# One list of single-engine steps for the norm stage and the first 17 products of a diffusion-transformer layer

## The chip, the cores and the metric

The kernel runs on one core of a Trainium2 chip. A core has TensorE (matrix products, PE in the profile; its weight loads are PEld), VectorE (DVE), ScalarE (ACT), GpSimd (POOL) and SyncE (SP, which here issues the DMA transfers). Each engine takes its instructions strictly in the order in which they were written for it and waits on semaphores for the others. The metric is the device time of one execution in microseconds (us); lower is better.

## The reference

One layer of a backbone over 1024 latent tokens and 256 context tokens, width 1024, float32. The part that matters here is the beginning:

```python
sh1, sc1, gt1, sh2, sc2, gt2 = [m[:, None] for m in adaln(c, w_mod[l], b_mod[l])]
csh1, csc1, cgt1, csh2, csc2, cgt2 = adaln(c_ctx, w_mod[l], b_mod[l])
h = modulate(rmsnorm(x, g_pre1[l]), sh1, sc1)
q, k, v, f, g_a, g_f = split_proj(h @ w_in[l])
```

`adaln` is `silu(c) @ w_mod + b_mod`, split in six; `rmsnorm` scales each token by the inverse root of its mean square; `modulate` is `h * (1 + scale) + shift`. Attention with a window, a Fourier branch, a merge and a gated feed-forward network follow.

## The kernel before

**Tiles.** A tile is 128 partitions by 512 float32, 256 KB. There are 40 such buffers of one tag (`s`, line 61), which hold x, the weights, the modulated activations and the halves of the operands; 8 PSUM banks (line 442); and ten tiles of three tile widths (`ha`), in which first the rows of `w_mod` (`ws`) lie, later the operands B21, T2, T3, T4n and B22. Until an operand is written its tile is lent to the weights of the six later modulation groups (`wa`, line 740).

**Products.** `h @ w_in` is done with Strassen-Winograd products, seven for each pair of output blocks. An operand on the activation side is a quarter of h, transposed (B11, B21, B22), or a difference of quarters (T1, T2, T3, T4n); on the weight side a quarter (A11 to A22) or a sum (S1 to S4). A float32 operand goes to TensorE as a high half (a cast by ScalarE, `copy`) and a low half (the remainder, a subtraction by VectorE); three matmuls of 128x512 replace one (`mm3`, line 83). A product has four K tiles, so 12 matmuls. The products have numbers: 0 to 2 are P1 of three weight pairs (operand B11), 3 to 5 P2 (B21), 6 to 8 P5 (T1), 9 to 11 P6 (T2), 12 to 14 P7 (T3), 15 and 16 P4 and P3 of the first pair (T4n, B22). P1, P6 and P7 of a pair add up in one PSUM bank (X), copied out after each; P5 and P3 use a bank Y, P2 a bank Z.

**The start, step by step.**
- `x_load` (line 477) loads two tiles per 128 tokens; `x_square` (502) squares and sums them on ScalarE; `x_norm` (511) makes the inverse root for two token tiles: two operations on VectorE, a root on ScalarE, five operations on VectorE; `x_scale` (536) scales a tile, on VectorE or ScalarE.
- `x_turn` (542) transposes one K tile of half the tokens on TensorE, four transposes into one bank.
- `wm_stage` (487) loads a quarter of the first 2048 columns of `w_mod`, eight transfers; `mod_rows` (569) multiplies them by `silu(c)`; `mod_copy` (577) copies the bank; `mod_turn` (582) turns it into columns; `mod_vec` (598) makes shift and scale for the latent (`c` = 0) or context (`c` = 1) stream, three small operations on VectorE.
- `x_mod` (551) modulates a turned K tile (`hr`), on VectorE or ScalarE; `x_put` (560) splits it into halves of an operand.
- `pre` loads weight quarters, `sums` adds them, `conv` splits them, `mm` does the matmuls (a range of K tiles), `evac` copies a bank out and `after` does what follows from it (sigmoid, store).
- `ada_load`, `ada_rows`, `ada_copy` (735 to 756) do a later group of modulation rows: 8 transfers, 16 matmul instructions, one copy. `warm` (591) fills waits of TensorE with transposes that nothing reads.

**What sets the order.** All of this is in a block with `tc.manual_schedule()` (lines 905 to 1129): each engine gets its instructions in the order of the calls. Helpers that touch two engines, such as `conv` and `x_put` (cast on ScalarE, then subtraction on VectorE), place both at once. Weight loads stand at the top (907 to 922), the rest in the order of the products. From product 17 on (`run(17, NI - 5)`, line 1130) a planner that simulates the engines orders the work.

Of the kernel before, what the change touches and what calls it, by code (L numbers as in the profile page):

```python
# [38 lines left out]

@with_exitstack  # L40
def block_kernel(ctx: ExitStack, tc: tile.TileContext, t: dict, out: bass.AP, dbg: dict):
# [469 lines left out]
    def x_norm(tk, fill=()):

        fill = list(fill)

        def between():
            if fill:
                fill.pop(0)()
# [6 lines left out]
        between()  # L524
        nc.vector.reciprocal(out=r, in_=sq)
        mul(n1, r, r)
        mul(n1, n1, v)
        between()
        nc.vector.tensor_scalar(out=n1, in0=n1, scalar1=-0.5, scalar2=1.5, op0=ALU.mult, op1=ALU.add)
        mul(r, r, n1)  # L530
        for t_ in range(2):
            xr_[tk + t_] = r[:, t_:t_ + 1]
        for f in fill:
            f()

    def x_scale(tk, h, eng):
        if eng is None:
# [37 lines left out]
            nc.tensor.matmul(modp[q][g:g + 32, :], sv32[:, k, :], wms[q, k], start=k < 4, stop=k >= 4, skip_group_check=True)
# [328 lines left out]
    run, lead, main, pre, conv, sums, mm, evac, after, st = wino(pairs, items, ps, hooks, seng=[nc.vector])  # L904
    with tc.manual_schedule():
        V = nc.vector
        for tk in range(4):
# [3 lines left out]
        pre(1, ("A11",))
        pre(2, ("A11",))
        wm_stage(1)
        for tk in range(4, 8):
            x_load(tk)
        wm_stage(2)
        for j in range(2):
            pre(j, ("A21", "A22"))
        wm_stage(3)
        for j in range(3):  # L920
            pre(j, ("A12",))
        pre(2, ("A21", "A22"))
        hb.update(hb_tiles(hbp, [o for o in OPS if o not in hb], 10))
        mov.update(moving(hb))

        for tk in range(2):
            x_square(tk)
        x_norm(0)
        for tk in range(2, 4):
            x_square(tk)  # L930
        for i in range(2):
            for tk in range(2):
                x_scale(tk, i, V)
        for k in range(4):
            x_turn(0, k, range(2))
        x_norm(2)
        mod_rows(0, range(4))
        for tk in range(2, 4):
            x_scale(tk, 0, V)
        for k in range(4):  # L940
            x_turn(0, k, range(2, 4))
        conv(0, "P1")
        for tk in range(2, 4):
            x_scale(tk, 1, V)
        mod_rows(0, range(4, 8))
        mod_copy(0)
        warm(6)
        mod_turn(0)
        mod_vec(0, 0)
        warm(8)  # L950
        for k in range(2):
            x_mod(0, k, V if k else None)
        mod_vec(0, 1)
        for k in range(2):
            x_put("B11", k, hraw[0, k])
        mm(0, range(2))
        conv(1, "P1")
        mm(1, range(2))
        conv(2, "P1")
        mod_rows(1, range(8))  # L960
        ada_load(0, range(KT))
        mod_copy(1)
        mm(2, range(2))
        mod_turn(1)
        mod_vec(1, 0)
        for k in range(2, 4):
            x_mod(0, k, V if k % 2 else None)
        x_turn(0, 4)
        x_turn(0, 5)
        mod_vec(1, 1)  # L970
        for k in range(2, 4):
            x_put("B11", k, hraw[0, k])
        warm(8)
        mm(0, range(2, 4))
        x_square(4)
        x_square(5)
        mm(1, range(2, 4))
        x_norm(4)
        for tk in (4, 5):
            x_scale(tk, 0, V)  # L980
        mm(2, range(2, 4))
        mod_rows(2, range(4))
        x_square(6)
        x_square(7)
        x_norm(6)
        for tk in (6, 7):
            x_scale(tk, 0, V)
        for j in range(3):
            evac(j)
        mod_rows(2, range(4, 8))  # L990
        ada_load(1, range(KT))
        mod_copy(2)
        for k in range(2):
            x_turn(1, k)
        mod_turn(2)

        def t1(k):
            sub(hraw[0, k], hraw[1, k], hraw[0, k])
            x_put("T1", k, hraw[0, k])

        for k in range(2):
            x_mod(1, k)
        mod_vec(2, 0)
        for k in range(2):
            x_mod(0, k + 4, V)
        for k in range(2, 4):
            x_turn(1, k)
        sums(0, "S1")
        for k in range(2):
            t1(k)  # L1010
        conv(0, "P5")
        sums(1, "S1")
        mod_rows(3, range(4))
        for k in range(2, 4):
            x_mod(1, k)
        mod_vec(2, 1)
        conv(1, "P5")
        mm(6, range(2))
        for k in range(2, 4):
            t1(k)  # L1020
        x_turn(0, 6)
        x_turn(0, 7)
        mm(7, range(2))
        for k in range(2):
            x_put("B21", k, hraw[0, k + 4])
        mod_rows(3, range(4, 8))
        ada_load(2, range(KT))
        rope_load()
        mod_copy(3)
        mm(6, range(2, 4))  # L1030
        mod_turn(3)
        mod_vec(3, 0)
        for k in range(2, 4):
            x_mod(0, k + 4, V if k % 2 else None)
        mm(7, range(2, 4))
        conv(0, "P2")
        mod_vec(3, 1)
        for k in range(2, 4):
            x_put("B21", k, hraw[0, k + 4])
        mm(3, range(2))  # L1040
        conv(1, "P2")
        for tk in range(4, 8):
            x_scale(tk, 1, None)
        mm(3, range(2, 4))
        conv(2, "P2")
        for k in range(4, 6):
            x_turn(1, k)
        sums(2, "S1")
        for k in range(4, 6):
            x_mod(1, k)  # L1050
        evac(3, True)
        mm(4)
        for k in range(6, 8):
            x_turn(1, k)

        def t2(k):
            sub(hraw[0, k], hraw[1, k + 4], hraw[0, k])
            x_put("T2", k, hraw[0, k])

        conv(2, "P5")  # L1060
        for k in range(2):
            t2(k)
        for k in range(6, 8):
            x_mod(1, k)
        evac(4, True)
        sums(0, "S3")
        sums(0, "S2")
        mm(5)
        for k in range(2, 4):
            t2(k)  # L1070
        conv(0, "P6")
        evac(5, True)
        mm(8)
        ada_rows(0, 0)
        ada_rows(0, 1)
        ada_copy(0)
        ada_load(3, range(KT))
        for j in range(1, 3):
            sums(j, "S3")
            sums(j, "S2")  # L1080
        mm(9)
        conv(1, "P6")
        conv(2, "P6")
        ada_rows(1, 0)
        ada_rows(1, 1)
        ada_copy(1)
        ada_load(4, range(KT))
        for j in range(4, 9):
            after(j)
        mm(10)  # L1090
        evac(9)
        ada_rows(2, 0)
        for k in range(4):
            sub(hraw[1, k], hraw[1, k + 4], hraw[1, k])
            x_put("T3", k, hraw[1, k])
        ada_rows(2, 1)
        ada_copy(2)
        ada_load(5, range(KT))
        mm(11)
        for j in range(3):  # L1100
            conv(j, "P7")
# [4 lines left out]
        mm(12)
        ada_rows(3, 0)
        ada_rows(3, 1)
        ada_copy(3)
        for k in range(4):  # L1110
            sub(hraw[0, k], hraw[0, k + 4], hraw[0, k])
            x_put("T4n", k, hraw[0, k])
        mm(13)
        ada_rows(4, 0)
        ada_rows(4, 1)
        ada_copy(4)
        mm(14)
        for k in range(4):
            x_put("B22", k, hraw[1, k + 4])
        for k in range(12, 15):  # L1120
            lead(k)
# [1120 lines left out]
```

## Time and profile before

| | us |
|---|---|
| median of 3 runs | 1343.81 (1343.79 to 1344.8) |
| the profiled execution | 1343.85 |
| its span in the profile | 1342.1 |
| mean granted clock of TensorE | 0.985 |
| DVE busy in the span | 1041.7 |
| ACT busy in the span | 679.0 |
| bytes moved from 0 to 134 us | 34.85 MB |

Times in the views are counted from the start of the span; 1.75 us of the profiled execution lie outside it. "Granted clock" is the share of full speed at which TensorE's array ran. In a timeline row the first number is the start, the second the duration; bracketed is the idle time of that engine before the row and what ended it. Durations of matmuls overlap, so the step from one start to the next is the better price.

### The profile page before, as it was taken

To read this page: it belongs to the slowest core of one execution; us is meant where nothing else is said; L and a number is where in the kernel's file an instruction comes from. 1 tells how busy PE (TensorE), PEld (TensorE's weight loads), DVE (VectorE), ACT (ScalarE), POOL (GpSimd) and SP (SyncE) were. 2 spreads that over 40 slices of the span, in tenths; PEclk is the share of its full clock that TensorE was granted. 3 is DMA by queue.
4 is the path that set the end of the run, shared out by engine and by line. 5 is a ranking of instruction groups with operands and counts; after the bars stand their busy time and mean duration, and the time that the engine had idled before them with its cause. 6 is when DMAs were issued, how large, how long until landed. Compare 5 with 4: busy or idle time off the path is not lost.

```text
span 1342.1 us, 18506 instructions
## 1 busy us (share of the span) xinstructions
PE 1277.3 (95%) x5998; PEld 1029.8 (77%) x5998; DVE 1041.7 (78%) x1899; ACT 679.0 (51%) x1349; POOL 231.5 (17%) x191
## 2 busy tenths in 40 slices
PE   6887999999999999999999999999999999999996
PEld 3554877788888887777876888888888887888885
DVE  3665576879498898677789999989987887666767
ACT  4545334642466776435467554545454445534442
POOL 0000030210044334100000013444555200000000
PEclk9798999999999999999999999999999999999998
DMA  9946546450613335663422287868676568987884
GB/s 311 354 160 213 169 153 218 145 149 20 190 53 114 120 113 154 212 227 110 134 72 63 82 240 228 243 196 258 208 230 192 176 209 280 375 271 226 284 289 147
DMA packets 271572, 254.55 MB, mean 190 GB/s; under 512 B 16732, under 2 KB 206836, under 8 KB 271476
## 3 DMA queue, kind: packets, MB, share of 16 engines
q1 hardware_dynamic: 271476, 253.38, 60.5%
q8 instruction: 47, 0.77, 0.2%
q14 instruction: 49, 0.40, 0.1%
HBM read 179.65 MB, written 73.40 MB: 189 GB/s over the span
## 4 chain that ended last, share of the span: by engine, by line
PE 69%; DVE 15%; ACT 6%; DMA 4%; issue 3%; SPq 1%; POOL 1%; DVEq 0%; ACTq 0%; POOLq 0%
PE X_u L87 5%; PE X_u L85 5%; PE X_u L86 5%; PE Y_u L85 3%; PE X_d L86 3%; PE X_d L87 3%; PE X_d L85 3%; PE Y_u L86 3%; PE Y_u L87 3%; PE X_g L85 2%; DVE p L1308 2%; PE X_g L86 2%; PE X_g L87 2%; DVE pl L68 2%; PE Y_d L85 1%
## 5 line engine op out<-in xcount | busy, mean ns | idle before, releaser
L68 DVE TENSOR_TENSOR lP_u<-A_u,hP_u 128x512 fp32r<-128x512 f32 x132 | 107.0, 815 | 23.0 <-ACT hP_u L307 21.3
L369 ACT COPY snP_u<-X_u 128x512 f32<-128x512 f32 x57 | 33.4, 586 | 131.7 <-PE X_u L87 131.6
L369 ACT COPY snP_d<-X_d 128x512 f32<-128x512 f32 x48 | 28.2, 587 | 98.5 <-PE X_d L87 95.2
L307 ACT CAST hP_u<-A_u 128x512 fp32r<-128x512 f32 x121 | 74.6, 619 | 0.0
L1328 POOL TENSOR_SCALAR p<-p,sm 128x640 f32<-128x640 f32 (+1 forms) x64 | 48.3, 775 | 91.9 <-PE pp L1333 44.9
L80 ACT CAST ph<-pp 128x512 fp32r<-128x512 f32 x76 | 44.3, 584 | 22.5 <-PE pp L1333 21.2
L68 DVE TENSOR_TENSOR pl<-pp,ph 128x512 fp32r<-128x512 f32 x76 | 51.7, 681 | 2.5 <-ACT ph L80 2.0
L1322 ACT ACTIVATE p<-p,nm 128x640 f32<-128x640 f32 (+1 forms) x64 | 51.4, 803 | 0.7 <-DVE nm L1315 0.7
L68 DVE TENSOR_TENSOR yd<-yd,snP_d 128x512 f32<-128x512 f32 x36 | 24.9, 691 | 34.3 <-ACT snP_d L369 34.2
L68 POOL TENSOR_TENSOR A_u<-A_u,A_u 128x512 f32<-128x512 f32 x28 | 47.9, 1710 | 13.9 <-DVE lP_u L68 6.1
L1308 DVE CUSTOM_DVE_ANT_0 p<-ss,mask 128x640 f32<-128x640 f32 (+1 forms) x64 | 49.9, 782 | 0.0
L1333 PE MATMUL pp<-ident,p 128*128 128x128 f32 x304 | 46.6, 274 | 2.8 <-POOL p L1328 1.5
L1333 PEld LDWEIGHTS pp<-ident,p 128*128 128x128 f32 x304 | 37.2, 140 | 11.6 <-POOL p L1328 2.9
L1743 DVE SCALAR_TENSOR_TENSOR tb<-u,vec,tb 128x1024 f32<-128x1024 f32 x22 | 39.5, 1796 | 3.1 <-ACT tb L1740 3.1
L68 DVE TENSOR_TENSOR lP_g<-A_g,hP_g 128x512 fp32r<-128x512 f32 x48 | 33.3, 701 | 8.6 <-ACT hP_g L80 8.6
L68 POOL TENSOR_TENSOR S_u<-A_u,A_u 128x512 f32<-128x512 f32 x14 | 24.2, 1730 | 87.8 <-DMA g_d0P<-ghP 81.7
L1304 PE MATMUL ss<-kst,qs 128*128 128x384 f32 (+1 forms) x128 | 36.6, 367 | 1.3 <-DVE mx L1308 0.8
L1744 DVE SCALAR_TENSOR_TENSOR tb<-u,vec,tb 128x1024 f32<-128x1024 f32 x22 | 36.5, 1658 | 0.9
L68 POOL TENSOR_TENSOR A_u<-S_u,A_u 128x512 f32<-128x512 f32 x14 | 18.7, 1338 | 104.1 <-DVE lP_u L68 104.1
L68 DVE TENSOR_TENSOR wB<-wB,wB 128x512 f32<-128x512 f32 x44 | 36.0, 818 | 0.0
L1344 PE MATMUL po<-pl,vst 128*128 128x512 f32 x76 | 31.3, 412 | 2.3 <-DVE pl L68 1.7
L1747 ACT ACTIVATE tb<-tb 128x1024 f32<-128x1024 f32 x22 | 23.4, 1063 | 16.6 <-DVE tb L1744 16.5
(884 smaller groups left out, 4383.1 us busy)
## 6 DMA issues: line engine op xcount, KB each, us to landing
A_u<-in_w_up SPq DMA_DIRECT2D x88, 256.0 KB, 4.5
wB<-in_w_down SPq DMA_DIRECT2D x44, 256.0 KB, 4.3
wa<-in_w_mod SPq DMA_DIRECT2D x36, 256.0 KB, 5.3
wt_dT<-wB SPq DMA_DIRECT2D x33, 256.0 KB, 2.6
wdB<-in_w_down SPq DMA_DIRECT2D x33, 256.0 KB, 4.7
wdT<-wt_dT SPq DMA_DIRECT2D x33, 256.0 KB, 2.9
A_g<-in_w_in SPq DMA_DIRECT2D x32, 256.0 KB, 5.9
ws<-in_w_mod SPq DMA_DIRECT2D x30, 256.0 KB, 6.1
```

The costliest lines, as they stand in the source:

```text
L68: return (eng or nc.vector).tensor_tensor(out=out, in0=a, in1=b, op=op)
L80: copy(hi, src)
L85: nc.tensor.matmul(ps, ah, bh, start=start, stop=False, skip_group_check=True)
L86: nc.tensor.matmul(ps, ah, bl, start=False, stop=False, skip_group_check=True)
L87: nc.tensor.matmul(ps, al, bh, start=False, stop=stop, skip_group_check=True)
L307: copy(st[j]["half", p][0], st[j][STA[p]])
L369: copy(d["s" + p], d["X"])
L1308: nc.vector.tensor_tensor_reduce(out=p_, in0=ssc[:, lo:768], in1=self.mk, op0=ALU.add, op1=ALU.max, scale=1.0, scalar=-3.0e38, accum_out=s ...
L1322: nc.scalar.activation(out=self.pt[g], in_=self.pt[g], func=AF.Exp, scale=SCALE, bias=self.m[:, g:g + 1], accum_out=self.sm[:, g:g + 1])
L1328: nc.gpsimd.tensor_scalar(out=self.pt[g], in0=self.pt[g], scalar1=self.sm[:, g:g + 1], scalar2=1.0, op0=ALU.mult, op1=ALU.mult)
L1333: nc.tensor.transpose(pp[:, g * P:(g + 1) * P], self.pt[g][:, j * P:(j + 1) * P], ident)
L1743: nc.vector.scalar_tensor_tensor(out=tb, in0=u[:, 0:1024], scalar=cw[0], in1=tb, op0=ALU.mult, op1=ALU.add)
```

## The change

The block's body is replaced by a table of named steps and a list of 384 names, `START_ORDER`, that is walked once. Most steps issue work for one engine; with few exceptions (`na`, `ev`, `af`, `ld`, `mark`) a step has one engine, and the rest of a helper is a step of its own. `conv` becomes `ch` (cast, ScalarE) and `cl` (subtraction, VectorE); `x_put` becomes `h` and `l`, with the difference `dT` apart; `x_norm` becomes `na` and `nb`; `x_turn` comes in halves (`tn03a`: token half 0, K tile 3, first two token tiles); `mod_rows` in halves (`rw0a`), its loads by two (`wq00`); a product by K tiles (`mm2.0`). `sc` and `md` are scaling and modulation on VectorE, `sa` and `ma` on ScalarE; `ca` is `mod_copy` on ScalarE; `l112` loads weight quarter A11 of pair 2; `S10` is the sum S1 of pair 0; `al`, `ar`, `ac` are the later modulation groups; `ev` and `el` evacuate, `el` leaves out what follows, which `af` does; `ld` and `mark` do what the planner's products need ahead. The calls are those of before, on the same tiles. Nine scalings instead of twelve are on VectorE, three modulations instead of five, and none of the four copies of `mod_copy`.

```diff
+START_ORDER = """
+xl1 l112 xl0 sq00 sq01 sq10 ch2P1 sq11 wq00 xl2 sq20 sq21 na0 xl3 xl4 sq30 sq31 xl6 sq40 xl5 sq41 nb0 sa11 sq50 na2 
+sc00 sc10 tn03a wu6 nb2 sc20 sq51 sq60 sa30 tn01a sq61 tn00a na4 nb4 xl7 wu8 tn02a sq70 wu8 wq02 tn02b wq04 wq06 rw0a 
+wq10 rw0b sc31 sq71 na6 nb6 tn01b cl2P1 sc60 sa40 wq12 wq14 sc70 sa50 tn12a wq16 sc01 tn10a tn03b ca0 mt0 sa51 tn00b 
+sc71 mv00 ma01 ma00 tn12b tn10b tn13a tn13b sc21 mv01 tn11a tn11b md10 tn06a tn06b tn04a tn04b hB110 lB110 l110 dT10 
+hB111 lB111 wq20 wq22 wq24 rw1a ma11 rw1b ca1 ch0P1 mm2.0 dT11 wq26 mt1 cl0P1 mm2.1 l111 mv10 ma02 hB112 mv11 hT11 
+mm0.0 lB112 tn05a tn05b ma03 l220 mm0.1 mm0.2 hB113 md13 md12 l210 wq30 lB113 mm2.2 hT10 rw2a rw2b wq32 wq34 wq36 
+sa61 dT13 hb mm2.3 sa41 tn15a lT11 ca2 mt2 mv20 mm0.3 hT13 tn15b ch1P1 cl1P1 ma05 dT12 mm1.0 tn16a S10 hT12 mm1.1 
+l222 mm1.2 mm1.3 ma04 ch0P5 S30 tn14a tn14b tn16b l121 lT10 cl0P5 mm6.0 hB211 mv21 hB210 tn17a tn17b rw3a rw3b mm6.1 
+l120 l122 lT13 ma15 lB211 ma14 lB210 dT20 ev1 lT12 S20 ca3 mt3 l211 l212 hT20 lT20 ch0P6 ch1P2 mm6.2 mv30 mv31 cl1P2 
+mm6.3 al0 tn07a ma06 dT21 hB212 lB212 ch2P2 cl2P2 ma16 dT22 tn07b ma07 mm4.0 mm4.1 ev0 ma17 mm5.0 ch0P2 S12 S32 mm4.2 
+hT21 cl0P2 mm5.1 mm5.2 ch2P5 hB213 lB213 S22 l221 mm3.0 mm3.1 al1 al2 mm5.3 hB223 mm3.2 mm3.3 cl2P5 mm4.3 ch2P6 cl2P6 
+cl0P6 ev2 mm8.0 mm8.1 S11 dT23 ch2P7 mm9.0 lT21 mm9.1 dT41 hT22 mm8.2 mm8.3 el3 af4 mm11.0 S40 S31 ch1P7 lT22 el5 
+ch0P7 mm11.1 el4 af5 ar1a ar1b S21 ar0a ar0b hT23 lT23 dT32 ar2a ac0 ch1P6 dT43 ch1P5 hT4n3 dT33 hT33 mm11.2 mm9.2 
+mm9.3 dT31 al3 al4 mm11.3 cl1P6 mm10.0 mm10.1 hT31 al5 mm10.2 dT40 af6 af7 af8 cl1P5 mm7.0 mm7.1 ev9 mm7.2 ac1 cl0P7 
+ar2b ar3a S42 ar3b cl2P7 mm10.3 dT30 hT30 hT32 ac3 lT30 cl1P7 S41 mark ev10 ac2 mm7.3 mm12.0 rope mm13.0 ev11 dT42 
+mm14.0 lT31 mm14.1 lT32 mm14.2 lT33 lB223 mm12.1 mm12.2 mm14.3 mm12.3 lT4n3 ev12 mm13.1 ld12 mm13.2 ld13 hT4n0 lT4n0 
+hB220 lB220 ar5a ar4a hT4n1 lT4n1 hB221 hT4n2 ar4b ac4 ar5b mm13.3 mm15.0 mm15.1 mm16.0 lB221 mm16.1 hB222 lB222 
+mm16.2 lT4n2 ev13 mm15.2 mm16.3 ld14 ld15 ld16 ev14 mm15.3 ev15 ac5 ev16
+"""
...
-    def mod_copy(q):
+    def mod_copy(q, put):
         rows = s(f"mc{q}")
-        nc.vector.tensor_copy(rows, modp[q])
+        put(rows, modp[q])
...
-        for tk in range(4):
-            x_load(tk)
-        pre(0, ("A11",))
-        wm_stage(0)
...
-        for k in range(15, 17):
-            lead(k)
-            mm(k)
-            evac(k)
+        steps = {}
+
+        def step_(name, fn, *a):
+            steps[name] = lambda: fn(*a)
...
+        def put_hi(o, k, src):
+            copy(mov[o][0][k], hraw[src])
+
+        def put_lo(o, k, src):
+            sub(mov[o][1][k], hraw[src], fbits(mov[o][0][k]))
+
+        def diff(a, b, c):
+            sub(hraw[a], hraw[b], hraw[c])
+
+        def conv_hi(j, p):
+            nm = pairs[j][2]
+            st[j]["half", p] = (s(f"h{p}_{nm}", R), s(f"l{p}_{nm}", R))
+            copy(st[j]["half", p][0], st[j][STA[p]])
+
+        def conv_lo(j, p):
+            st[j][p] = hi, lo = st[j].pop(("half", p))
+            sub(lo, st[j][STA[p]], fbits(hi))
...
+            step_(f"ca{q}", mod_copy, q, lambda o, i: copy(o, i))
...
+        for name in START_ORDER.split():
+            steps[name]()
     run(17, NI - 5)
```

More of the change, by code (lines that the diff above doesn't have):

```diff
@@ L485, in wm_quarter, with wm_stage @@
              in_=w_mod[k * P:(k + 1) * P, :2 * D].rearrange("p (w c) -> p w c", w=2)[:, :, q * 256:(q + 1) * 256])
-    def wm_stage(q):
-        for k in range(KT):
+    def wm_stage(q, ks):
+        for k in ks:
             i = q % 2 * 8 + k
@@ L509, in block_kernel, with x_norm @@
     xss, xr_ = {}, {}
[L511 to L517, printed above, removed]
+    x_rest = {}
+    def x_norm(tk):
         ss, nm = xss[tk], f"x{tk}"
@@ L523, in x_norm, with second @@
         nc.scalar.activation(out=sq, in_=v, func=AF.Sqrt)
[L524 to L534, printed above, removed]
+        def second():
+            nc.vector.reciprocal(out=r, in_=sq)
+            mul(n1, r, r)
+            mul(n1, n1, v)
+            nc.vector.tensor_scalar(out=n1, in0=n1, scalar1=-0.5, scalar2=1.5, op0=ALU.mult, op1=ALU.add)
+            mul(r, r, n1)
+            for t_ in range(2):
+                xr_[tk + t_] = r[:, t_:t_ + 1]
+        x_rest[tk] = second
     def x_scale(tk, h, eng):
@@ L906, in block_kernel @@
         V = nc.vector
-        for tk in range(4):
-            x_load(tk)
-        pre(0, ("A11",))
-        wm_stage(0)
[L911 to L933, printed above, removed]
-        for k in range(4):
[L935 to L1101, printed above, removed]
@@ L1102, in block_kernel @@
-        evac(10)
-        evac(11)
-        for k in range(-12, 12):
-            lead(k)
[L1106 to L1121, printed above, removed]
-            evac(k)
@@ L1123, in block_kernel, with hb_more @@
-        ada_rows(5, 0)
-        ada_rows(5, 1)
-        ada_copy(5)
-        for k in range(15, 17):
-            lead(k)
-            mm(k)
-            evac(k)
+        steps = {}
+        def step_(name, fn, *a):
+            steps[name] = lambda: fn(*a)
+        def hb_more():
+            hb.update(hb_tiles(hbp, [o for o in OPS if o not in hb], 10))
+            mov.update(moving(hb))
+        def put_hi(o, k, src):
+            copy(mov[o][0][k], hraw[src])
+        def put_lo(o, k, src):
+            sub(mov[o][1][k], hraw[src], fbits(mov[o][0][k]))
@@ new lines, in diff, with square @@
+        def diff(a, b, c):
[7 more added lines that the diff above has]
+            sub(lo, st[j][STA[p]], fbits(hi))
+        def square(tk, i):
+            if tk % 2 == 0 and i == 0:
+                xss[tk] = tiny(f"ss{tk}", 4, 16)
+            nc.scalar.activation(out=junk, in_=xs[tk][i], func=AF.Square, accum_out=xss[tk - tk % 2][:, tk % 2 * 2 + i:tk % 2 * 2 + i + 1])
@@ new lines, in block_kernel @@
+        for tk in range(8):
+            step_(f"xl{tk}", x_load, tk)
+            for i in range(2):
+                step_(f"sq{tk}{i}", square, tk, i)
+                step_(f"sc{tk}{i}", x_scale, tk, i, V)
+                step_(f"sa{tk}{i}", x_scale, tk, i, None)
+        for tk in range(0, 8, 2):
+            step_(f"na{tk}", x_norm, tk)
+            step_(f"nb{tk}", lambda tk=tk: x_rest.pop(tk)())
+        for j in range(4):
+            for a in ("11", "12", "21", "22"):
+                step_(f"l{a}{j}", pre, j, ("A" + a,))
+            for p in MOV:
+                step_(f"ch{j}{p}", conv_hi, j, p)
+                step_(f"cl{j}{p}", conv_lo, j, p)
+            for o in ("S1", "S2", "S3", "S4"):
+                step_(f"{o}{j}", sums, j, o)
@@ new lines, in block_kernel @@
+        for q in range(4):
+            for k in range(0, 8, 2):
+                step_(f"wq{q}{k}", wm_stage, q, range(k, k + 2))
+            step_(f"rw{q}a", mod_rows, q, range(4))
+            step_(f"rw{q}b", mod_rows, q, range(4, 8))
+            step_(f"cp{q}", mod_copy, q, nc.vector.tensor_copy)
+            step_(f"ca{q}", mod_copy, q, lambda o, i: copy(o, i))
+            step_(f"mt{q}", mod_turn, q)
+            for c in range(2):
+                step_(f"mv{q}{c}", mod_vec, q, c)
+        step_("hb", hb_more)
@@ new lines, in block_kernel @@
+        step_("rope", rope_load)
+        for h in range(2):
+            for k in range(8):
+                step_(f"tn{h}{k}a", x_turn, h, k, range(2))
+                step_(f"tn{h}{k}b", x_turn, h, k, range(2, 4))
+                step_(f"md{h}{k}", x_mod, h, k, V)
+                step_(f"ma{h}{k}", x_mod, h, k, None)
+        src = {"B11": lambda k: (0, k), "B21": lambda k: (0, k + 4), "T1": lambda k: (0, k), "T2": lambda k: (0, k),
+               "T3": lambda k: (1, k), "T4n": lambda k: (0, k), "B22": lambda k: (1, k + 4)}
@@ new lines, in block_kernel @@
+        for o in src:
+            for k in range(4):
+                step_(f"h{o}{k}", put_hi, o, k, src[o](k))
+                step_(f"l{o}{k}", put_lo, o, k, src[o](k))
+        for k in range(4):
+            step_(f"dT1{k}", diff, (0, k), (1, k), (0, k))
+            step_(f"dT2{k}", diff, (0, k), (1, k + 4), (0, k))
+            step_(f"dT3{k}", diff, (1, k), (1, k + 4), (1, k))
+            step_(f"dT4{k}", diff, (0, k), (0, k + 4), (0, k))
+        for i in range(17):
+            for k in range(4):
+                step_(f"mm{i}.{k}", mm, i, range(k, k + 1))
+            step_(f"ev{i}", evac, i)
+            step_(f"el{i}", evac, i, True)
+            step_(f"af{i}", after, i)
+            step_(f"ld{i}", lead, i)
@@ L1130, in block_kernel @@
+        for g in range(6):
+            step_(f"al{g}", ada_load, g, range(KT))
+            step_(f"ar{g}a", ada_rows, g, 0)
+            step_(f"ar{g}b", ada_rows, g, 1)
+            step_(f"ac{g}", ada_copy, g)
+        step_("mark", lambda: [lead(k) for k in range(-12, 12)])
+        for n in (2, 4, 6, 8):
+            step_(f"wu{n}", warm, n)
+        for name in START_ORDER.split():
+            steps[name]()
     run(17, NI - 5)
```

## The prediction

> **What bounds the kernel now.** I read the page first, then the busy time by stretch, then TensorE's timeline over the first 140 us, and last the timelines of ScalarE and VectorE where TensorE waits.
>
> ```profile
> span 1342.1 us, 18506 instructions
> ...
> PE 1277.3 (95%) x5998; PEld 1029.8 (77%) x5998; DVE 1041.7 (78%) x1899; ACT 679.0 (51%) x1349; POOL 231.5 (17%) x191
> ...
> PE   6887999999999999999999999999999999999996
> ...
> PEclk9798999999999999999999999999999999999998
> ...
> GB/s 311 354 160 213 169 153 218 145 149 20 190 53 114 120 113 154 212 227 110 134 72 63 82 240 228 243 196 258 208 230 192 176 209 280 375 271 226 284 289 147
> ```
>
> PE is busy 95% of the span, and the only digits below 9 (but for the last) are the first four slices of 33.55 us each. The changed list lies there. The next rows, busy time by stretch, give length, PE, PEld, DVE, ACT and POOL busy, then the granted clock, DMA share and GB/s.
>
> ```profile
> 23.78:133.74 109.96, 90.43 (x428) 58.39 (x429) 63.99 (x127) 54.76 (x103) 0.00 (x0) 0.86 0.76 255
> ...
> 133.74:1342.10 1208.36, 1175.75 (x5515) 965.45 (x5513) 967.99 (x1736) 611.65 (x1219) 231.21 (x186) 1.00 0.59 182
> 50.00:60.00 10.00, 7.25 (x28) 5.01 (x28) 6.87 (x14) 5.47 (x10) 0.00 (x0) 0.56 1.06 380
> ```
>
> The first product starts at 23.78, and product 17, the first after the list, at 133.74. Between them PE idles 109.96 - 90.43 = 19.5 us, and the clock of 0.86 costs 0.14 x 109.96 = 15.4 more: 34.9 us lost of 110. VectorE and ScalarE are busy 64 and 55 us there, so neither is full. From 133.74 on PE idles 32.6 us in 1208 at full clock, so what the start gains should reach the end.
>
> TensorE's timeline shows where it is lost (start, duration, engine, line, what; in brackets the idle time before and what ended it):
>
> ```profile
> 53.52 0.79 PE L85 MATMUL Y_g<-T1a,hP_g 128*128 128x512 f32 x1 [2.75 <-ACT hP_g L80]
> 54.11 0.63 PE L86 MATMUL Y_g<-T1a,hP_g 128*128 128x512 f32 x1
> 54.54 0.63 PE L87 MATMUL Y_g<-T1a,lP_g 128*128 128x512 f32 x1
> ...
> 78.75 0.50 PE L85 MATMUL Z_g<-B21a,hP_g 128*128 128x512 f32 x1 [4.13 <-ACT hr L555]
> ...
> 104.73 0.80 PE L85 MATMUL X_g<-T3a,hP_g 128*128 128x512 f32 x1 [4.09 <-ACT hP_g L80]
> ...
> 126.45 0.50 PE L85 MATMUL X_g<-T4na,hP_g 128*128 128x512 f32 x1 [4.28 <-ACT snP_g L297]
> ```
>
> Four waits make 15.25 of the 19.5 us. Each starts a new operand (T1, T2, T3, T4n), and after it matmuls step by 0.43 us (54.11 to 54.54). The reason is the hand-over in the two other engines:
>
> ```profile
> 50.35 0.62 ACT L80 CAST T1a<-hr 128x512 fp32r<-128x512 f32 x1 [3.91 <-DVE hr L68]
> 52.33 0.62 ACT L80 CAST T1a<-hr 128x512 fp32r<-128x512 f32 x1 [1.36 <-DVE hr L68]
> ```
>
> ```profile
> 51.00 0.69 DVE L68 TENSOR_TENSOR T1a<-hr,T1a 128x512 fp32r<-128x512 f32 x1 [0.68 <-ACT T1a L80]
> 51.61 0.68 DVE L68 TENSOR_TENSOR hr<-hr,hr 128x512 f32<-128x512 f32 x1
> ```
>
> Difference, cast, low half, next difference: 52.33 - 50.35 = 1.98 us per K tile, both engines waiting in turn. A K tile takes PE 0.68 us (below), so PE runs dry at each new operand.
>
> **The change, part by part.** No instruction is added, and the list gives every engine its order. The casts go between other work, each operand's K tiles are prepared one or two products ahead, and a product is cut where its next tile isn't ready. Prices at full clock:
>
> ```profile
> 32.16 0.95 PE L586 MATMUL pm<-sel,mc 128*128 128x2 f32 x8
> 32.97 0.63 PE L547 MATMUL x<-ident,x 128*128 128x128 f32 x4
> ...
> 40.08 1.92 PE L575 MATMUL mr<-ws,sv 128*32 128x512 f32 x16
> 41.94 0.44 PE L547 MATMUL x<-ident,x 128*128 128x128 f32 x2
> ...
> 73.24 1.37 PE L547 MATMUL x<-ident,x 128*128 128x128 f32 x8
> ...
> 110.08 1.48 PE L751 MATMUL ar<-wa,sv 128*32 128x512 f32 x10
> ...
> 111.94 0.50 PE L85 MATMUL X_g<-T3a,hP_g 128*128 128x512 f32 x1
> ...
> 133.74 0.39 PE L85 MATMUL X_g<-T4na,hP_g 128*128 128x512 f32 x1
> ...
> 136.46 0.39 PE L85 MATMUL Y_g<-B22a,hP_g 128*128 128x512 f32 x1
> ```
>
> A product takes 136.46 - 133.74 = 2.72, a K tile 0.68; a row group (`rw`, two halves) 41.94 - 40.08 = 1.86; an `ar` pair 111.94 - 110.08 = 1.86; `mt` 32.97 - 32.16 = 0.81; a turn of a K tile 1.37 / 2 = 0.68.
>
> *When the first product starts.* In the list `mm2.0` stands behind `rw1b` on PE, which needs `wq16`. In SP's order all eight `xl` (16 transfers), `l112`, `wq00` to `wq16` (16) come first: 33 transfers of 0.262 MB and 0.14 MB of constants, 8.8 MB. Before, the first product needed only 17. This is the list's price. The bytes moved so far:
>
> ```profile
> 0.00:30.00 30.00, 17.06 (x80) 9.72 (x84) 12.17 (x41) 14.11 (x31) 0.31 (x5) 0.94 0.96 306
> 0.00:37.00 37.00, 23.17 (x119) 14.48 (x120) 15.65 (x51) 17.38 (x38) 0.31 (x5) 0.95 0.98 314
> 0.00:46.50 46.50, 30.75 (x162) 19.29 (x163) 20.32 (x70) 24.91 (x57) 0.31 (x5) 0.95 1.01 316
> ```
>
> 9.2 MB by 30.0, 11.6 by 37.0, 14.7 by 46.5. With some lag for transfers in flight I take 30.5 for the first product, 6.7 later than before. `rw2` (42 transfers, 11.1 MB) can run by 37, `rw3` (53, 14.0 MB) by 46.5. ScalarE is not later than the loads: 16 squares, 7 scalings and the casts ahead of `hB110` start about a microsecond after the 7.02 of before (x1 and `l112` are now loaded ahead of x0) and end near 28, by these rows:
>
> ```profile
> 7.02 0.61 ACT L507 ACTIVATE junk<-x 128x512 f32<-128x512 f32 x1
> ...
> 7.75 0.63 ACT L507 ACTIVATE junk<-x 128x512 f32<-128x512 f32 x1
> ...
> 66.55 2.57 ACT L538 ACTIVATE x<-x,rx 128x512 f32<-128x512 f32 x4
> ```
>
> (16 x 0.73 + 7 x 0.64 = 16.2; six casts and modulations near 0.6 add 3.6, and the four roots wait for VectorE.)
>
> *What PE has left then.* 68 K tiles 46.2; `rw2` and `rw3` 3.7; three `mt` 2.4; six turns (05, 15, 16, 14, 17, 07) 4.1; six `ar` pairs 11.2. Sum 67.6, so without any wait product 17 starts at 30.5 + 67.6 = 98.1. (A check: before did the 68 K tiles, three row groups 5.6, three `mt`, twelve turns 8.2 and the `ar` after 23.78, 73.6 and some warm-ups; 109.96 - 34.9 = 75.) The ten other turns, both early row groups and all 22 warm-ups lie ahead of 30.5, beside the loads.
>
> *What is late next.* I walked the list with these prices. (a) By 30.5 PE has trickled behind loads, so one slow stretch is likely. One in 50 to 60 cost at most 0.44 x 7.25 busy us = 3.2; part of it now falls while PE waits for loads anyway, so I take 2. (b) `mm0.0` needs a PSUM bank that `ma02` frees, and `ma02` needs `mt1`: about 1. (c) VectorE. From `rw3b` to `ar1a` it has 30 operations, each 0.61 in a run (51.00 to 51.61), and two vector steps of about 0.5: 19.3 us. PE has 23 K tiles, one turn and one `mt` there, 17.1. So PE loses 2; VectorE catches up while PE does `ar1`, `ar0` and half of `ar2`. Together 5 us: 103.1.
>
> Bounds of what before does not show: waits of casts and loads for one of 40 tiles `s`, eight banks, ten tiles `ha`. Below: nothing, or a gain, as a tile comes free earlier. Above: the longest wait of PE in the list, 4.28, with its 2.0 of slow clock, at three places: 6.3 x 3 = 19. I take the near end, since the list delays the loads that would fill the tiles (`l211` to `l221` behind `rw3`). After 133.74 `run(17, ...)` is ordered by the planner, whose clock starts elsewhere; its order may shift by up to the 32.6 us idle there. I take nothing, plus or minus 3.
>
> *Sum.* 133.74 - 103.1 = 30.6 earlier. The profiled execution's own time is 1343.85 (span 1342.1 and 1.75 around it), the median 1343.81, so 1343.85 - 30.6 = **1313.2 us**.
>
> A rule that speaks against it: the Trainium skill, "TensorE: Matmul & The Clock Gate", section "A second HAM failure mode: psum-queue depth-cycling", says that frequent small idle gaps between groups of matmuls make the clock swing between half and full. Its Part 1 puts the drop at one idle window of about 3.4 us; here 2.75 us were enough (53.52), so the measurement decides, and short gaps are not safe. By the first rule the many cuts could keep the clock low; that is rival C.
>
> **The rivals.**
>
> *B, the spare tiles set the pace.* The gate rows' weights `al0` to `al5` borrow operand tiles; SP is one queue.
>
> ```profile
> SPq L742 <- PE ar L751: 33.3, 3, 20.5
> ```
>
> SP waited 33.3 us for `ar` to free them. In the list `al0` follows `rw3`, `al3` and `al4` follow `ar0` and `ar1`, and `al5` must wait for tiles that `ar3` frees (those of `ar0` and `ar1` went to `al3` and `al4`); 13 K tiles (8.8 us) hide it before `ar5a`. If each of three turnovers leaves PE 4.28 idle and 2.0 slow, 19 us: 122, saved 11.7, **1332**. For: single queue, `ar` now near its loads. Against: in the third and fourth slice of the page DMA moves 160 and 213 GB/s, after 311 and 354, so there is room.
>
> *C, slower: the clock stays low.* If waits under a microsecond keep half clock through the list, each K tile steps by 0.43 x 3 = 1.29 instead of 0.68: 68 x 0.61 = 41.5, and the other 21.4 us of PE work lose as much in proportion, 19: 98.1 + 60.5 = 158.6, 24.9 later, **1369**. It decides from 35.6 of those 60.5 us on, that is when 6 in 10 of the work runs slow. Against: before has 0.86 with gaps of 4 us.
>
> *D, nothing is won.* The planner's order after product 17 gives it back: 30 us, as much as all idle time there; **1343**. Nothing in the profile speaks for it.
>
> *E, better.* No wait at all and the planner gains 3: **1305**.
>
> **How the numbers follow.** Forecast (product 17 at 98 to 109, 1308 to 1319) 0.60; B and lesser forms of it (1319 to 1335) 0.24; E 0.07; C 0.06; D 0.03. Range 1305 to 1331 leaves out C, D, B's upper end and some of E, near 0.18. Faster by over 0.2% (2.7 us, about what a measurement of this kernel can tell from no change): 0.91; within it 0.03; slower 0.06.
>
> **What would show it.** The first X_g matmul near 30.5, and before it transposes of both halves. The first product after the list (X_g from T4na, then kv) near 103. Between them PE idle below 5 us, no single wait over 2, granted clock above 0.95. VectorE and ScalarE without pairs of 1.4 and 0.7 us waits. SP waiting for `ar`, but with PE not waiting for wa. The stretch after unchanged at 1208 within 3. It is wrong if PE waits for a wa load or `ha` tile (B), if matmuls step by 0.43 us with short gaps (C), or if the last stretch grows (D).

## The result and the profile after

| | before | after |
|---|---|---|
| median | 1343.8 (1343.5 to 1344.8, 4 runs) | 1312.14 (1310.59 to 1312.75, 4 runs) |
| the profiled execution | 1343.85 | 1312.6 |
| its span | 1342.1 | 1310.8 |
| mean granted clock of TensorE | 0.985 | 0.996 |

The ratio is 0.9761, with a 95% interval of 0.9744 to 0.9778: 31.7 us faster at the medians, 31.3 between the two profiled executions. The page of after, first its busy times, then the rows of its 40 slices (32.77 us each) that were shown of before:

```profile
span 1310.8 us, 18510 instructions
...
PE 1260.3 (96%) x5998; PEld 1022.7 (78%) x5998; DVE 1034.5 (79%) x1890; ACT 683.3 (52%) x1358; POOL 231.5 (18%) x191
...
PE   5999999999999999899999999999999999999996
...
PEclk9999999999999999999999999999999999999998
...
GB/s 314 352 328 222 143 219 147 192 21 162 59 113 112 127 131 128 267 154 153 89 41 97 148 255 208 225 219 221 250 185 211 196 210 296 370 262 226 285 283 148
```

TensorE does the same 5998 matmuls. The 8, 8 and 7 that the second to fourth slice of before had, and the 7 and 8 of their clock, are gone. The first slice is lower than before (5, not 6), since the first product comes later; a new 8 in the 17th slice is the merge stage (see below). The loads, which dropped to 160 GB/s in the third slice of before, now run at 314, 352 and 328 for three slices. TensorE's timeline of after gives the two ends of the list (start, duration, engine, line, what):

```profile
30.85 0.59 PE L594 MATMUL mr<-wm,sv 128*32 128x512 f32 x1
31.37 0.50 PE L108 MATMUL X_g<-B11a,hP_g 128*128 128x512 f32 x1
...
99.92 0.39 PE L108 MATMUL X_g<-T4na,hP_g 128*128 128x512 f32 x1
```

The first product starts at 31.37 and product 17 at 99.92 (133.74 before): 33.8 us earlier. Busy time by stretch (length, then PE, PEld, DVE, ACT, POOL busy with counts, granted clock, DMA share, GB/s) shows how full TensorE is between them, and what comes after:

```profile
31.37:99.92 68.55, 68.53 (x381) 46.30 (x381) 51.54 (x99) 45.85 (x80) 0.00 (x0) 1.00 1.02 341
99.92:1310.80 1210.88, 1175.82 (x5515) 965.18 (x5513) 969.58 (x1740) 613.78 (x1223) 231.17 (x186) 1.00 0.59 183
```

Of 68.55 us TensorE idles 0.02, at full clock. Between these two products no wait is left to fill; ahead of the first, TensorE is still idle for half the time (31.37 us, 15.97 of them busy). The stretch behind it is 2.5 us longer than the 1208.36 of before: 33.8 won, 2.5 given back, 31.3.

**Where the 2.5 go.** The starts of the last 5515 matmuls of two traces, matched one by one from the end, tell how far ahead each kernel is at any place. TensorE's lead over the profiled execution of before, in us, at five of its times, all counted from each trace's first matmul (the other rows are experiments of the next section):

```
lead over before      at 351.8   at 523.7   at 545.0   at 619.6   at the end
after                   33.85      32.95      32.71      31.50      31.33
list                    35.48      34.45      33.95      33.35      33.32
nowarm                  34.07      34.06      33.45      31.42      31.45
wpafirst                33.76      32.90      32.57      33.68      33.63
wpafirst2               34.31      30.47      30.01      31.21      31.25
pairs                   14.31      14.34      14.28      14.62      14.52
before_wpa               0.66       0.55      -0.62       1.02       0.84
```

After product 17 the lead is constant for 218 us, and from 620 on it is constant again. It is lost at two places. The first is at 352 to 367 of before, 320 to 330 of after, TensorE's timeline of after:

```profile
324.38 0.39 PE L110 MATMUL Y_g<-B22b,lP_g 128*128 128x512 f32 x1
325.55 2.05 PE L1125 MATMUL pab<-c,fd 128*128 128x128 f32 x16 [0.79 <-DVE c_g L91]
```

Before, these transposes followed the last product without a wait; now there are 0.79 us, because VectorE, which makes `c_g`, stands ahead of it at another step (`nsnk`, line 1087) and waits 3.65 us there, up to 324.61, for the load of `snk`. In before that wait was 1.54. The earlier start alone doesn't bring the loss: nowarm, as far ahead, loses nothing here. The second is the merge stage, where the rows of TensorE and of SP's queue belong together:

```profile
549.69 0.79 PE L108 MATMUL pa<-ah,whpa 128*128 128x512 f32 x1 [3.29 <-ACT whpa L1483]
550.28 0.63 PE L109 MATMUL pa<-al,whpa 128*128 128x512 f32 x1
550.71 0.63 PE L110 MATMUL pa<-ah,wlpa 128*128 128x512 f32 x1
```

```profile
535.37 0.32 SPq L1329 DMA_DIRECT2D sga<-sga_d  x1
543.00 0.32 SPq L1329 DMA_DIRECT2D mf<-mf_d  x1
543.42 1.47 SPq L1459 DMA_DIRECT2D wor<-in_w_out  x1
544.98 0.39 SPq L1249 DMA_DIRECT2D wpa<-in_w_pa  x1
```

SP issues one load at 535.37 and the next, `mf`, only at 543.00, because `mf` needs one of eleven buffers that VectorE still has in use. The load of `w_pa`, which has a buffer, stands behind it and is issued at 544.98; TensorE, which wanted it at 546.4, waits 3.29 us and then steps by 0.43 us for 3.4 us. The stop of SP is not new. In SP's queue of before it is nearly as long, 7.13 us instead of 7.63:

```profile
568.39 0.45 SPq L1438 DMA_DIRECT2D sga<-sga_d  x1
575.52 0.32 SPq L1438 DMA_DIRECT2D mf<-mf_d  x1
```

There TensorE's waits for `whpa` were 0.31 and 1.58 us; after has one of 3.29, list has 3.9 us in two. Before also ran at half clock for 3.4 us in its merge stage (from 553.7), list not at all.

### The profile page after: what moved, and what is told of

It reads as the page before. It is cut to its first block, busy times and chain, and to the rows that moved or that the text cites. A ratio compares the mean times of both kernels' runs of the same rounds, so it can differ in the third digit from the quotient of the medians.

```text
span 1310.8 us, 18510 instructions
## 1 busy us (share of the span) xinstructions
PE 1260.3 (96%) x5998; PEld 1022.7 (78%) x5998; DVE 1034.5 (79%) x1890; ACT 683.3 (52%) x1358; POOL 231.5 (18%) x191
## 4 chain that ended last, share of the span: by engine, by line
PE 73%; DVE 15%; ACT 4%; DMA 3%; issue 3%; SPq 1%; POOL 1%; DVEq 0%; POOLq 0%; ACTq 0%
PE X_u L110 5%; PE X_u L108 5%; PE X_u L109 5%; PE X_d L110 3%; PE X_d L109 3%; PE X_d L108 3%; PE Y_u L108 3%; PE Y_u L110 3%; PE Y_u L109 3%; PE X_g L108 2%; PE X_g L110 2%; PE X_g L109 2%; DVE p L1199 2%; DVE pl L91 2%; PE Y_d L108 1%
## 5 line engine op out<-in xcount | busy, mean ns | idle before, releaser
L91 POOL TENSOR_TENSOR S_u<-A_u,A_u 128x512 f32<-128x512 f32 x14 | 24.7, 1763 | 88.6 <-DMA g_d0P<-ghP 81.7
L91 DVE TENSOR_TENSOR lP_g<-A_g,hP_g 128x512 fp32r<-128x512 f32 x48 | 33.3, 701 | 5.3 <-ACT hP_g L103 4.3
L1235 PE MATMUL po<-pl,vst 128*128 128x512 f32 x76 | 31.3, 411 | 2.6 <-DVE pl L91 2.0
L320 ACT COPY snP_g<-X_g 128x512 f32<-128x512 f32 x24 | 14.1, 588 | 36.4 <-PE X_g L110 35.6
```

What stands on the lines that cost most here:

```text
L91: return (eng or nc.vector).tensor_tensor(out=out, in0=a, in1=b, op=op)
```

## Experiments

My theory: before loses its time because VectorE does difference, low half, next difference of one K tile at a time and so alternates with ScalarE's casts; the list wins by the order of each engine, above all VectorE's, and by cutting products where a tile isn't ready. The rivals: the win is the moving of work from VectorE to ScalarE; or the clock, held up by warm-ups or lost by cuts; or the order of the loads. "Before" in each row is the kernel before on the same chip, 1343.54 to 1343.73.

| run | median us | ratio to before (95%) |
|---|---|---|
| pairs | 1331.33 | 0.9908 (0.9895 to 0.9922) |
| uncut | 1319.03 | 0.9814 (0.9801 to 0.9828) |
| pairs_uncut | 1337.89 | 0.9959 (0.9944 to 0.9974) |
| batch2 | 1330.19 | 0.9898 (0.9884 to 0.9911) |
| engines | 1314.24 | 0.9783 (0.9770 to 0.9797) |
| nowarm | 1312.15 | 0.9764 (0.9751 to 0.9777) |
| loads | 1323.54 | 0.9849 (0.9834 to 0.9863) |
| list (the changed kernel again) | 1312.95 | 0.9773 (0.9760 to 0.9787) |
| wpafirst | 1310.15 | 0.9746 (0.9731 to 0.9761) |
| wpafirst2 (the same again) | 1311.04 | 0.9759 (0.9746 to 0.9773) |
| before_wpa | 1342.38 | 0.9991 (0.9982 to 1.0000) |

**pairs: VectorE's order alone.** In the list each low half goes back directly behind its cast and each difference directly ahead of it. TensorE's, ScalarE's and SP's orders stay as they are. An excerpt:

```diff
-hB110 lB110 l110 dT10 hB111 lB111 wq20 wq22 wq24 rw1a ma11 rw1b ca1 ch0P1 mm2.0 dT11 wq26 mt1 cl0P1 mm2.1
-l111 mv10 ma02 hB112 mv11 hT11 mm0.0 lB112
+hB110 lB110 l110 hB111 lB111 wq20 wq22 wq24 rw1a ma11 rw1b ca1 ch0P1 cl0P1 mm2.0 wq26 mt1 mm2.1
+l111 mv10 ma02 hB112 lB112 mv11 dT11 hT11 lT11 mm0.0
```

> The changed list, with each pair put together again: every subtraction that makes a low half stands right behind its cast, and each difference right ahead of it; TensorE's order is untouched. If the gain comes from splitting the pairs, VectorE gets 45 waits of about 0.65 us (29 us) on top of 71 busy in 110 and becomes the bound: product 17 starts 10 to 20 us later than the 99.9 of the changed kernel, 1322 to 1332. If it comes from preparing operands early and VectorE's free 28% takes up the waits: within 3 of 1312.

Measured 1331.33: 19.2 us of the 31.7 are gone by VectorE's order alone, with the first product where it was (30.95). The hand-over of before is back, in ScalarE's, VectorE's and TensorE's timelines of this run:

```profile
49.75 0.62 ACT L936 CAST T1a<-hr 128x512 fp32r<-128x512 f32 x1 [1.37 <-DVE hr L91]
```

```profile
50.40 0.69 DVE L91 TENSOR_TENSOR T1a<-hr,T1a 128x512 fp32r<-128x512 f32 x1 [0.69 <-ACT T1a L936]
```

```profile
69.48 0.50 PE L108 MATMUL Z_g<-B21b,hP_g 128*128 128x512 f32 x1 [2.30 <-ACT B21b L936]
```

1.37 and 0.69 are before's 1.36 and 0.68. Of the 19.2 us about 5 are clock, by an estimate from two windows: 0.83 from 40 to 60 us and 0.91 from 60 to 80. In after the four casts of T1 and its four low halves lie like this (the rows of T1 alone, other work between them left out), ScalarE first:

```profile
35.01 0.62 ACT L936 CAST T1a<-hr 128x512 fp32r<-128x512 f32 x1
36.86 0.61 ACT L936 CAST T1a<-hr 128x512 fp32r<-128x512 f32 x1
39.86 0.62 ACT L936 CAST T1b<-hr 128x512 fp32r<-128x512 f32 x1
42.83 0.62 ACT L936 CAST T1a<-hr 128x512 fp32r<-128x512 f32 x1 [0.43 <-DVE hr L91]
```

```profile
38.51 0.69 DVE L91 TENSOR_TENSOR T1a<-hr,T1a 128x512 fp32r<-128x512 f32 x1
44.04 0.69 DVE L91 TENSOR_TENSOR T1a<-hr,T1a 128x512 fp32r<-128x512 f32 x1
45.61 0.68 DVE L91 TENSOR_TENSOR T1b<-hr,T1b 128x512 fp32r<-128x512 f32 x1
48.02 0.68 DVE L91 TENSOR_TENSOR T1a<-hr,T1a 128x512 fp32r<-128x512 f32 x1
```

In these rows neither engine waits for the other, but for 0.43 once: when VectorE takes up a low half, its cast has been done for 2.9 to 6.6 us. Not every operand is as far ahead: VectorE still waits for casts now and then up to 100 us, 1.2 us at the longest, but none of these waits reaches TensorE.

**batch and batch2: before, with T1, T2, T3 and T4n in groups.** Nothing of the list; only the K tiles of these four operands are prepared in groups of two or four. In `batch` the two operands of the differences are exchanged, so T1, T2, T3 and T4n have the opposite sign; `batch2` has them as before.

```diff
-        for k in range(4):
-            sub(hraw[1, k], hraw[1, k + 4], hraw[1, k])
-            x_put("T3", k, hraw[1, k])
+        for k in range(4): sub(hraw[1, k], hraw[1, k + 4], hraw[1, k])
+        for k in range(4): copy(mov["T3"][0][k], hraw[1, k])
+        for k in range(4): sub(mov["T3"][1][k], hraw[1, k], fbits(mov["T3"][0][k]))
```

> The kernel before, with one part of the change alone: for T1, T2, T3 and T4n the differences of a group of K tiles come first, then their casts, then their low halves, so that the two engines work side by side; no step moves otherwise. Four tiles then take about 5.4 us instead of 7.9. If the hand-over is what TensorE waited for, each of the four waits (15.2 us in all) shrinks by up to 2.5 and some slow stretches go: 1329 to 1336. If only preparing operands a product ahead helps: 1341 or more.

> The kernel before with the K tiles of T1, T2, T3 and T4n in groups of two or four (all differences, then all casts, then all low halves), operands in the order of before. If the alternation of cast and subtraction sets the four long waits of before (2.75, 4.13, 4.09, 4.28): 1329 to 1336, and waits before T1, T2, T3 and T4n that are shorter by 1 to 3 us each. If the place of an operand (one or two products ahead) is what counts and grouping does nothing: 1342 to 1345.

Measured 1330.46 and 1330.19, so grouping alone wins 13.5 us. TensorE's timeline of batch2 at the first matmul of T1, of product 5 (Z, operand B21) and of T4n:

```profile
51.43 0.79 PE L85 MATMUL Y_g<-T1a,hP_g 128*128 128x512 f32 x1 [1.38 <-ACT hP_g L80]
...
74.22 0.50 PE L85 MATMUL Z_g<-B21a,hP_g 128*128 128x512 f32 x1 [2.75 <-ACT hr L555]
...
112.95 0.50 PE L85 MATMUL X_g<-T4na,hP_g 128*128 128x512 f32 x1 [2.47 <-ACT snP_g L297]
```

Before's waits of 2.75, 4.13 and 4.28 are 1.38, 2.75 and 2.47 here, and the one of 4.09 ahead of T3 is gone: 15.25 us have become 6.6. The rest of the 13.5 is clock (0.91 from the first product to product 17, where before has 0.86) and smaller waits. So the alternation is tried from both sides: put back into the list it costs 19.2, taken out of before it wins 13.5. The two are not the same set of steps. `pairs` puts back every low half, of weights too, and every difference; `batch2` groups only the 16 K tiles of T1 to T4n.

**uncut: products whole.** All four K tiles of a product stand where the list has its last one.

```diff
-mm0.0 lB112 tn05a tn05b ma03 l220 mm0.1 mm0.2 hB113 md13 md12 l210 wq30 lB113 mm2.2 hT10 rw2a rw2b
-wq32 wq34 wq36 sa61 dT13 hb mm2.3
+lB112 tn05a tn05b ma03 l220 hB113 md13 md12 l210 wq30 lB113 hT10 rw2a rw2b
+wq32 wq34 wq36 sa61 dT13 hb mm2.0 mm2.1 mm2.2 mm2.3
```

> The changed list with the products whole: the four K tiles of each stand where the last one stood; the rest is untouched. If the cuts are needed as filler between the row groups that wait for loads, PE idles about 4 us between rw1 and rw2 and runs one slow stretch: 1316 to 1319. If tiles are ready early enough for whole products: within 2 of 1312.

Measured 1319.03, 6.9 us worse than after: the upper end. The start shows how, in TensorE's timeline of uncut:

```profile
32.72 4.85 PE L594 MATMUL mr<-ws,sv 128*32 128x512 f32 x16 [0.21 <-PE x L566]
37.50 0.50 PE L108 MATMUL X_g<-B11a,hP_g 128*128 128x512 f32 x1
```

Row group 2 takes 4.85 us instead of the 1.86 of an undisturbed one, since TensorE waits for its loads four times in it (2.70 us), and the first product waits behind it until 37.50. Up to half of the 6.9 is clock: half speed for 3.4 us from 33.35 and again from 60.66. In the list six K tiles of products 0 and 2 stand ahead of that row group and fill the time. A cut product is thus filler for waits on loads; with them filled, the clock of the list stays at 1.00.

**pairs_uncut: both undone.**

> The changed list with both undone: pairs together and products whole. If the two are separate terms, the loss is the sum of the losses of each alone. If one covers the other (uncut products need split pairs less, or more), it differs from the sum by over 3 us. What then is still won against before is the share of order across products and of the load order.

Measured 1337.89, 25.75 us worse than after; the single losses add up to 19.2 + 6.9 = 26.1. The two are additive, and what the rest of the list (the order across products, the loads, the engines) wins over before is 1343.73 - 1337.89 = 5.8.

**engines: the work back on the engines of before.** Copies of `mod_copy` on VectorE, scalings and modulations divided as before, all at the list's places.

```diff
-sa11 sa30 sa40 sa50 sc71 ca0 ca1 ca2 ca3 ma01 ma03 ma05 ma07 ma04 md10 md12 md13
+sc11 sc30 sc40 sc50 sa71 cp0 cp1 cp2 cp3 md01 md03 md05 md07 md04 ma10 ma12 ma13
```

> The changed list with the engines of before: the four copies of mod_copy, four more scalings and two more modulations (net) back on VectorE, in the same places. If only the order matters: within 2 of 1312. If taking work off VectorE is what pays, it gets 5 us more in a stretch where it is near 80% busy: 1316 to 1318.

Measured 1314.24, 2.1 us worse, about as much as the runs of one kernel spread; its trace agrees, with product 17 at 102.18 instead of 99.92. The longest waits of TensorE in the list are 0.2 to 0.6, and the clock from 31 to 100 stays at 1.00. So the division of work is worth 2 of 31.7.

**nowarm: without the 22 warm-up transposes.** `wu6 wu8 wu8` are left out.

> The changed list without the 22 warm-up transposes, whose results nothing reads. If they keep the clock up, the first products run at half clock for one stretch: 1314 to 1315, with steps of 0.43 us from 31 on. If transposes and row groups are enough: 1312 and a granted clock of 1.00 from 31 on.

Measured 1312.15, the same as after. Busy time of this run from 15 us on:

```profile
15.00:31.00 16.00, 14.09 (x80) 7.47 (x80) 10.14 (x39) 12.42 (x30) 0.00 (x0) 1.00 1.09 354
31.00:100.00 69.00, 68.98 (x385) 46.42 (x382) 52.13 (x99) 45.86 (x80) 0.00 (x0) 1.00 1.03 336
```

The clock of 1.00 in the first of these rows counts only from 24.65 on, where the clock records of this run begin. TensorE's timeline of the run shows what was granted ahead of that, by eight transposes each:

```profile
15.37 2.15 PE L566 MATMUL x<-ident,x 128*128 128x128 f32 x8 [11.31 <-DVE x L559]
...
24.86 1.09 PE L566 MATMUL x<-ident,x 128*128 128x128 f32 x8
```

At 15.37 they take twice as long as at 24.86, so without the warm-ups full speed comes by 24.7. In after, with them, it comes at 20.6: eight transposes take 1.89 us at 18.87 and 1.04 at 20.82. The four us cost nothing, as they lie ahead of the first product, and up to there loads set the pace: DMA share 1.09, and the first product at 31.16, 0.2 earlier than with the 22.

**loads: the 36 load steps in the order of before, at the top.**

> The changed list with the 36 load steps of x, w_mod and w_in in the order of before, at the top. x4 to x7 then land near 31 us instead of 17, and ScalarE's squares of them stand ahead of the copy and modulations: if the load order is part of the gain, the first product starts near 36 instead of 31.4 and the time is 1317 to 1320. If waiting for 17 transfers instead of 33 is worth more: below 1312.

Measured 1323.54: the direction as expected, 3.5 us above the upper end. The cause is another than the one I had in mind. ScalarE's, VectorE's and TensorE's timelines of this run:

```profile
20.18 0.62 ACT L947 CAST hP_g<-A_g 128x512 fp32r<-128x512 f32 x1 [10.63 <-DMA A_g<-in_w_in]
```

```profile
24.74 0.88 DVE L559 TENSOR_SCALAR x<-x,rx 128x512 f32<-128x512 f32 x2
```

```profile
25.28 0.87 PE L566 MATMUL x<-ident,x 128*128 128x128 f32 x2 [21.10 <-DVE x L559]
```

`ch2P1`, the cast of A11 of pair 2, is ScalarE's fourth step in the list, which is safe there because `l112` is the second load. With before's loads that tile comes behind ten other load steps; ScalarE waits 10.63 us at the cast with 13 of the 16 squares queued behind it, and norm, turn and first product (at 41.85 instead of 31.37) are as late. From there product 17 is 68.62 us away, as in after, so all of the loss lies ahead of the first product. So this run doesn't price the load order by itself; it shows that load order and ScalarE's order are one choice. A load order that is tested apart from it was not tried.

**wpafirst, with list and before_wpa beside it.** In the merge stage the load of `w_pa` is issued ahead of the two loads of `pa_load`.

```diff
         pa_mm(j, h, ps(f"pa{j}{h}"))
+        w_next = i % 2 == 0 and 4 <= i // 2 + 2 < KT
+        if w_next:
+            raw, m = merge_raw(t["w_pa"], i // 2 + 2, "pa"), i // 2 + 2
         if i + 3 < len(PA) and PA[i + 3] not in pal:
             pa_load(*PA[i + 3], so)
...
-        if i % 2 == 0 and 4 <= i // 2 + 2 < KT:
-            raw, m = merge_raw(t["w_pa"], i // 2 + 2, "pa"), i // 2 + 2
+        if w_next:
             paw[m] = s(f"whpa{m}", R), s(f"wlpa{m}", R)
```

> The changed kernel, and in the merge stage each load of a w_pa tile placed ahead of the two loads of the gate and Fourier tiles that wait for a buffer on the same queue. Of the 33.8 us won by product 17, 2.5 are lost again, and the trace shows PE waiting 3.3 us for whpa there. If that queue is the cause: 1308 to 1310.5. If that stage is bound by the bytes it moves: 1312.

> The changed kernel once more, on the same chip as the next run, to compare the two directly: 1310 to 1313.5.

> The changed kernel with the load of w_pa issued ahead of the next pa_load in the merge stage, beside the changed kernel on one chip. If the queue of SP in the merge stage takes 2 of the 2.5 us that are given back: 1.5 to 3 us below the run list, and no wait over 1 us for the halves of w_pa. If the first comparison (1310.15 against 1312.14) was a difference between chips: within 0.7 of list.

> The kernel before with the same edit of the merge stage. If the wait arises only with the phase that the list brings: within 1 us of before. If the queue costs the same without the list: 2 us or more below before, 1341.8 or less.

The edit gives 1310.15 against 1312.14, and beside the changed kernel on one chip 1311.04 against 1312.95: 1.9 to 2.0 us twice, though the single runs overlap (1309.81 to 1312.68 against 1310.77 to 1313.91) and so do the intervals of the ratios. The table of leads is clearer, since it looks at the place itself: from 545.0 on, where the edit can act, to 619.6 after, list and nowarm lose 1.21, 0.60 and 2.03 us, the two runs with the edit gain 1.11 and 1.20. That no wait above 1 us would be left was wrong; TensorE's waits of wpafirst2 from 540 to 570 us (in total, times, longest):

```profile
PE pa L108 <- ACT whpa L1485: 2.5, 1, 2.5
```

In list the same view has 3.9 us in two waits. One of two is gone: `mf` still stops SP for its buffer, and a later load of the stage still stands behind it. In before the edit is worth 1.64 us by the leads from 545.0 on, in one trace, and 1.3 by the medians, where the interval of the ratio reaches 1.0000. (By 523.7 it looks like 0.5, since this trace has a wait of 1.22 us at 539.99, ahead of the edit's place.) So the edit wins about 2 us in the changed kernel, 1.7 to 3.2 by the leads, and most of that in before too: as far as these traces show, SP's queue costs both kernels, and the earlier start adds little to that cost. The edit thus more than makes up for the loss in this stage, but the queue isn't shown to be what brought the loss. What the 2.5 us come from stays open in the main: the unedited runs lose 0.6 to 2.0 us here, and 0 to 1.0 at 352 us, where nothing was tried. `pairs`, only 14.3 us ahead of before, loses nothing at either place.

## Why the prediction was right, step by step

The forecast was 1313.2, the median 1312.14. Its steps:

- **The bound** held: the two losses of the start, idle TensorE and clock, are gone, and most of the gain reaches the end.
- **First product at 30.5.** 31.37 in after and 29.77 to 31.34 in the other runs with the whole list; loads pace it, as nowarm shows. The estimate from bytes was 0.9 early here.
- **67.6 us of TensorE's work behind it.** 68.55 measured with 0.02 idle: the sum of the prices was 0.95 (1.4%) too low.
- **5 us of stalls: mis-sized, it was none.** (a) No slow clock stretch: 1.00 throughout. (b) No wait for the bank of `ma02`. (c) VectorE's shortfall never reached TensorE. I had counted 19.3 us of VectorE between `rw3b` and `ar1a` against 17.1 of TensorE's, as if TensorE needed each result at once; the list prepares one or two products ahead, and that margin covers 2 us: VectorE takes up the first of these operations, `lT13`, at 45.61, 3.3 us before TensorE's first at 48.93. With the two steps above, 99.92 = 103.1 + 0.87 + 0.95 - 5.
- **Nothing for waits on `s` tiles, banks and `ha` tiles.** Right for TensorE, and the waits exist, off its path. In after, the waits of SP up to 134 us and of VectorE from 16 to 100 us have

```profile
SPq L761 <- PE ar L770: 6.5, 4, 4.7
```

```profile
DVE T3a L91 <- PE ar L770: 4.6, 1, 4.6
```

  VectorE waits 4.6 us for a tile that is lent to the weights of `ar`, and TensorE does not notice. SP's wait for `ar` fell from 33.3 to 6.5.
- **The later part unchanged, plus or minus 3.** It lost 2.5: inside the bound, at two places that I had not named. I expected the planner's order to be what shifts. The rows show waits on loads and clock instead, and SP's queue for a buffer, which before has as well; how much is lost differs from run to run, and the cause stays open in part.

So the sum came within about a microsecond of the median partly by luck, through two errors of opposite sign: product 17 was 3.2 us earlier than forecast, and 2.5 were given back. Rival B did not come: SP waits for `ar`, TensorE for no `wa` load. Rival C did not come. The rule behind it (the Trainium skill, "TensorE: Matmul & The Clock Gate", "A second HAM failure mode: psum-queue depth-cycling") speaks of idle gaps between groups of matmuls, and the cuts left no gaps: they removed them, so this run does not test it. Of D, 2.5 of 33.8 us came true. E had no waits, which was right, and a gain of the planner, which was not.

Three readings of the prediction do not hold in the rows of before, though the sum does not hang on them.

- **Not every one of the four waits starts a new operand.** The second, 4.13 at 78.75, is the first matmul of product 5, whose operand B21 had been in use for two products. It waits for a PSUM bank that a modulation on ScalarE frees (`hr`, line 555), and that one is queued behind the paired casts of T2. T2's own first product, at 87.90, needed no wait.
- **The hand-over reaches TensorE by way of ScalarE's queue.** All four brackets name ScalarE, and none of them a cast of T1 to T4n: twice the cast of a weight's high half (`hP_g`), once that modulation, once the copy of a bank (`snP_g`). In ScalarE's queue each of these stands behind paired casts.
- **The 2.75 us at 53.52 did not bring the clock down.** It had been at half since 45.1, and the wait ahead of that was 1.86:

```profile
44.23 1.32 PE L547 MATMUL x<-ident,x 128*128 128x128 f32 x6 [1.86 <-DVE x L540]
45.34 1.75 PE L586 MATMUL pm<-sel,mc 128*128 128x2 f32 x8
```

  Eight such matmuls take 0.95 us at 32.16. That short gaps are not safe stands, and all the more.

## What to carry to other kernels

Where two engines hand a tile to and fro (difference, cast, remainder), the order within one engine decides: let each work through several tiles before it takes up what depends on the other; here that was 19 of 32 us. Cut a long operation into pieces where it can fill waits on loads, and set the order of loads and of the engine that uses them first together. Look in every stage for a queue in which a load that waits for a buffer stands ahead of one that doesn't; here that was worth about 2 us, and 1.3 to 1.6 in before.
